# Attention values as plain fp32 products, row sums on VectorE

## The chip, the cores and the metric

The kernel runs on one core of a Trainium2 chip. The metric is the device time of one execution in microseconds (us). The kernel before took 1972.14 us as the median of three runs (1970.95 to 1979.14). The profiled execution took 1971.03 us. The engines are called as the profile calls them: PE is TensorE (PEld its weight loads), DVE is VectorE, ACT is ScalarE, POOL is GpSimd, and SP issues most of the transfers.

## The reference, cut to what matters

Two layers run one after the other on 1024 positions of width 1024. The change lies in the second layer, in a latent attention with 8 heads; everything else is left out here.

```python
def odd_layer(x, cos, sin, g_pre, g_post, w_in, g_q, w_uq, g_kv, w_ukv, w_fd, w_out):
    ...
    k_nope, v = kv[..., :QK_NOPE], kv[..., QK_NOPE:]      # 128 and 128 columns per head
    ...
    def attend(qs):
        qn, qr = qs
        s = jnp.einsum('bqhd,bkhd->bhqk', qn, k_nope) + jnp.einsum('bqhr,bkr->bhqk', qr, k_rope)
        pr = jax.nn.softmax(s.astype(jnp.float32) * scale, axis=-1).astype(v.dtype)
        return jnp.einsum('bhqk,bkhd->bqhd', pr, v)
    ...
    y = jnp.concatenate([y_c, y_d], axis=-1) @ w_out
    return x + rms_norm(y, g_post)
```

## The kernel before

Products of fp32 matrices are made of three products in the type fp32r. Each operand is split into a high part, rounded to fp32r, and a low part, the rest. `mm3` then multiplies high by high, high by low and low by high, all into one sum in PSUM. The split `split_act_dve` is a copy on ACT (the high part) and a subtraction on DVE (the low part); `wload` splits weights on ACT or POOL.

The attention goes through the heads `h` and, for each, through 8 tiles of 128 keys (`kt`). One tile of work is 128 keys by 1024 queries. The loop is skewed: in the pass for head `h` PE makes the scores of head `h` (`scores`), and for the head before, `h - 1`, the exponentials (`weigh`) and the products with the values (`values`) are made. `scores` leaves a score tile in PSUM, which ACT copies to `st` and DVE folds into a running maximum `acc`. After eight tiles `maxima` turns `acc` on PE, reduces it on DVE to `sm`, and spreads it over the partitions as `mb`. `weigh` subtracts `mb` (DVE, line 1741), takes the exponential `e` (ACT, line 1742), adds `e` to the row sums `es` (POOL, lines 1745 and 1747), and splits `e` into `eh` and `el` (ACT line 201, DVE line 202). `values` makes two times three products of 512 columns into the PSUM tiles `c` and `d` (lines 196 to 198). `finish` multiplies by a gate into `zt`, sums `es` over the partitions on PE (line 1772), takes the reciprocal (`rsum`, line 1774), and stores the head's output. `v_page` makes the values of a pair of heads, split into `vh` and `vl`. `prep_q`, `prep_k` and `prep_r` make the queries and keys of the next head; their weights are split on POOL (lines 180 and 181).

For head 7 there are no further scores. The scheduler puts a part of the output projection beside it: products `mm<-wh,yh`, with the splits of its weights on POOL (`wl`, line 210) and of its inputs on DVE (`yl`), and with sums and differences of blocks on DVE (`s`, `a`, `b`, lines 303 and 306) and POOL. The rest of the projection follows, then the last normalization and the stores.

A scheduler with a model of times sets the order on each engine when the kernel is built. Each engine then runs its list in that order, and so does SP with the transfers.

Of the kernel before, what the change touches and what calls it, by code (L numbers as in the profile page):

```python
# [8 lines left out]
F32 = mybir.dt.float32  # L9
F32R = mybir.dt.float32r  # L10
I32 = mybir.dt.int32
BF16 = mybir.dt.bfloat16
AF = mybir.ActivationFunctionType
ALU = mybir.AluOpType
AX = mybir.AxisListType

P = 128
S = 1024
D = 1024
NT = S // P  # L20
# [10 lines left out]
NEG = -(2.0 ** 100)  # L31
SB = 3
ST_BUFS = 9
E_BUFS = 3
ES_BUFS = 1
EH_BUFS = 2
PTS = [6]*7+[2]
EB = 3
CB = 6
# [40 lines left out]
def hybrid_encoder(ctx: ExitStack, tc: tile.TileContext, d):  # L80
    nc = tc.nc
    V, A, PL, T = nc.vector, nc.scalar, nc.gpsimd, nc.tensor
# [23 lines left out]
    def nm(s):  # L106
        uid[0] += 1
        return f"{s}_{uid[0]}"
# [60 lines left out]
    def wload(src, n, bufs=None, pool=None, tags=("wh", "wl")):  # L169

        raw = wr_pool.tile([P, w_cols], F32, tag="wr", name=nm("wr"))[:, :n]
        pool = pool or wpool
        m = w_cols if tags[0] == "wh" else n
        hi = pool.tile([P, m], F32R, tag=tags[0], bufs=bufs, name=nm("wh"))[:, :n]
        lo = pool.tile([P, m], F32R, tag=tags[1], bufs=bufs, name=nm("wl"))[:, :n]
        nc.sync.dma_start(out=raw, in_=src)
        if w_act[0]:
            A.activation(hi, raw, AF.Copy)
        else:
            PL.tensor_scalar(out=hi, in0=raw, scalar1=1.0, scalar2=1.0, op0=ALU.mult, op1=ALU.mult)  # L180
        PL.tensor_tensor(out=lo, in0=raw, in1=f(hi), op=ALU.subtract)
        return hi, lo
# [12 lines left out]
    def mm3(out, lh, ll, rh, rl, start, stop, shared=False):  # L195
        T.matmul(out, lh, rh, start=start, stop=False, skip_group_check=shared)  # L196
        T.matmul(out, lh, rl, start=False, stop=False, skip_group_check=shared)  # L197
        T.matmul(out, ll, rh, start=False, stop=stop, skip_group_check=shared)  # L198

    def split_act_dve(hi, lo, src):  # L200
        A.activation(hi, src, AF.Copy)  # L201
        V.tensor_tensor(out=lo, in0=src, in1=f(hi), op=ALU.subtract)  # L202
# [179 lines left out]
    wv, fu_w = [], []  # L382
# [16 lines left out]
    for half in range(2):  # L399
# [10 lines left out]
        pt = c_tile()  # L410
# [9 lines left out]
        pt = c_tile()  # L420
        for j in range(4):
            T.matmul(pt[:, j * P:(j + 1) * P], rsh[:, 4 * half + j:4 * half + j + 1].broadcast_to([P, P]),
                     ident, start=True, stop=True)
# [711 lines left out]
    for k in range(NK):  # L1135
        pt, g = x1_cols(ysb1, k)
# [8 lines left out]
    for i in range(n):  # L1145
        w = w_load(0, k2[i])
# [477 lines left out]
    def v_page(h, q):  # L1624

        pr = h // 2
        if pr not in wv:
            wv[pr] = (wload(d["wv"][pr * P:(pr + 1) * P, :], 512, 1, None, ("whv", "wlv")), [], [])
        w, vh, vl = wv[pr]
        pt = a_tile()  # L1630
        for j in range(2):
            tt = 2 * q + j
            for k in range(2):
                mm3(pt[:, j * 256:(j + 1) * 256], tt_slices(ckh[k], tt), tt_slices(ckl[k], tt),
                    w[0][:, k * 256:(k + 1) * 256], w[1][:, k * 256:(k + 1) * 256], k == 0, k == 1)
        vh.append(at.tile([P, 512], F32R, tag="vh", bufs=4, name=nm("vh")))
        vl.append(at.tile([P, 512], F32R, tag="vl", bufs=4, name=nm("vl")))
        split_act_dve(vh[q], vl[q], pt)

    def load_w(h, *parts):  # L1640

# [84 lines left out]
            A.activation(mb[:, i * 512:(i + 1) * 512], pt, AF.Copy)  # L1726
        s_["mb"] = mb

    def e_parts(e):
        eh = at.tile([P, S], F32R, tag="eh", bufs=EH_BUFS, name=nm("eh"))  # L1730
        el = at.tile([P, S], F32R, tag="el", bufs=EH_BUFS, name=nm("el"))
        split_act_dve(eh, el, e)
        return eh, el

    def weigh(h, kt):

        s_ = hd[h]
        st = s_["st"][kt]
        sc = st
        st = at.tile([P, S], F32, tag="e", bufs=E_BUFS, name=nm("e"))  # L1740
        V.tensor_tensor(out=st, in0=sc, in1=s_["mb"], op=ALU.subtract)  # L1741
        A.activation(st, st, AF.Exp, scale=scale)  # L1742
        if kt == 0:
            s_["es"] = at.tile([P, S], F32, tag="es", bufs=ES_BUFS, name=nm("es"))
            PL.tensor_scalar(out=s_["es"], in0=st, scalar1=1.0, scalar2=1.0, op0=ALU.mult, op1=ALU.mult)
        else:
            PL.tensor_tensor(out=s_["es"], in0=s_["es"], in1=st, op=ALU.add)  # L1747
        s_["eh"], s_["el"] = e_parts(st)

    def values(h, kt):  # L1750
        s_ = hd[h]
        if kt == 0:
            s_["po"] = [c_tile(), d_tile()]
        _, vh, vl = wv[h // 2]
        vs = slice((kt % 2) * 256 + (h % 2) * P, (kt % 2) * 256 + (h % 2 + 1) * P)
        for i in range(2):
            qs = slice(i * 512, (i + 1) * 512)
            mm3(s_["po"][i], vh[kt // 2][:, vs], vl[kt // 2][:, vs], s_["eh"][:, qs], s_["el"][:, qs],
                kt == 0, kt == NT - 1)

    def finish(h):

# [79 lines left out]
    with ExitStack() as os_:  # L1842
# [10 lines left out]
            return yp.tile([P, 512], F32, tag=tag, bufs=bufs, name=nm(tag))  # L1853

        def junk1():
            return at.tile([P, 512], BF16, tag="vh", bufs=4, name=nm("junk"))


        acc0 = op_acc(0)
# [33 lines left out]
            third(i)  # L1893
        second(n - 1)
        third(n - 1)
        gp1 = at.tile([P, D], F32, tag="eh", bufs=EH_BUFS, name="gp1")
        nc.sync.dma_start(out=gp1, in_=d["g_post1"].broadcast_to([P, D]))
        ss1, ss2 = (small.tile([P, 8], F32, tag="oss", name=nm("oss")) for _ in range(2))
        for j in range(4):
# [31 lines left out]
        for i in range(n):  # L1931
            w = w_load(0, k1[i])
            sub(V, w, b11[i], w)
            t = at.tile([P, S], F32, tag=("el", "el", "eh")[i], bufs=EH_BUFS, name=nm("a22"))
            a22.append([t[:, 0:512], t[:, 512:1024]])
            for r in range(2):
                y_load(2 * k2[i] + r, 1, a22[i][r])
                sub(V, a11[i][r], a22[i][r], a11[i][r])
            block(w, a11[i], acc0, i)
# [22 lines left out]
        for j in range(4):  # L1962
            ts_ = slice(j * P, (j + 1) * P)
            for i in range(n):
                for r in range(2):
                    cs = slice(r * 512, (r + 1) * 512)
                    mm3(acc1[j], ys[i][r][0][:, ts_], ys[i][r][1][:, ts_], ws_[i][0][:, cs], ws_[i][1][:, cs],
                        i + r == 0, i == n - 1 and r == 1)
            t = ysb2[j]
            add(t[:, f0], t[:, f0], acc1[j])  # L1970
            junk = at.tile([P, 512], BF16, tag="vh", bufs=4, name=nm("junk"))
            A.activation(junk, t[:, f0], AF.Square, accum_out=ss2[:, j:j + 1])
            s1 = small.tile([P, 1], F32, tag="oss2", name=nm("oss2"))
            V.tensor_tensor(out=s1, in0=ss2[:, j:j + 1], in1=ss2[:, 4 + j:5 + j], op=ALU.add)
            PL.tensor_tensor(out=t[:, f0], in0=t[:, f0], in1=gp1[:, f0], op=ALU.mult)
            rs = rms_scale(s1, 1, D)
            for cs in (f0, f1):
                V.scalar_tensor_tensor(out=t[:, cs], in0=t[:, cs], scalar=rs, in1=xr[j][:, cs],
                                       op0=ALU.mult, op1=ALU.add)
                nc.scalar.dma_start(out=d["out"][(4 + j) * P:(5 + j) * P, cs], in_=t[:, cs])  # L1980
# [130 lines left out]
```

## Time and profile before

| | |
|---|---|
| median of three runs | 1972.14 us (1970.95 to 1979.14) |
| profiled execution | 1971.03 us |
| its span | 1969.3 us |
| PE busy | 1795.7 us, 91% |
| DVE busy | 1511.4 us, 77% |
| ACT busy | 775.2 us, 39% |
| POOL busy | 759.4 us, 39% |
| chain that ended last | PE 60%, DVE 23%, issue 8%, DMA 5%, POOL 2%, ACT 2% |

The span is the profiled stretch of that execution. Busy shares are averages over stages with different limits, so the stage of the change has to be read by itself. A matmul's record is longer than the time until the next one starts, because matmuls are pipelined; what a matmul costs is read from one start to the next. The granted clock of PE stands as a share of 2.4 GHz; the two levels are 1.2 and 2.4 GHz.

### The profile page before, as it was taken

What the parts mean: (1) busy time and instruction counts of PE and PEld (TensorE: products, weight loads), DVE (VectorE), ACT (ScalarE), POOL (GpSimd) and SP (SyncE); (2) the same over time, 40 slices, a digit from 0 to 9 for tenths busy, and PEclk for the clock granted to TensorE, in tenths of its full rate; (3) what the DMA queues carried; (4) which work ended last, traced back from release to release, by engine and by line L of the source; (5) the groups of instructions that cost most, each with busy time, mean ns of one, the idle gap of its engine ahead of it and who ended that gap; (6) DMA issues with size and microseconds to landing.
All of it is one profiled execution on the core that took longest, in us unless ns stands there. A gap on an engine that the chain in (4) does not pass through costs nothing.

```text
span 1969.3 us, 22736 instructions
## 1 busy us (share of the span) xinstructions
PE 1795.7 (91%) x8204; PEld 1422.6 (72%) x8204; DVE 1511.4 (77%) x2260; ACT 775.2 (39%) x1217; POOL 759.4 (39%) x453
## 2 busy tenths in 40 slices
PE   6999999999999999988967999989989898987786
PEld 6988888888888777766855787768667676665564
DVE  7597757698776257788788879656787978899788
ACT  5322232233232334434455323342555545564232
POOL 3432231323221114127554332331454545467343
PEclk8999999999999999989978999999999999998898
DMA  4333232313312515675235134463001001033423
GB/s 156 119 106 120 75 97 73 99 54 105 112 63 75 192 49 183 218 273 177 86 132 207 59 114 154 146 202 110 13 18 58 15 30 34 32 133 107 155 76 128
DMA packets 99491, 214.34 MB, mean 109 GB/s; under 512 B 10098, under 2 KB 31091, under 8 KB 99251
## 3 DMA queue, kind: packets, MB, share of 16 engines
q1 hardware_dynamic: 66610, 158.69, 24.9%
q10 hardware_dynamic: 32768, 54.21, 7.3%
q8 instruction: 64, 1.05, 0.2%
q14 instruction: 49, 0.39, 0.1%
HBM read 154.47 MB, written 58.39 MB: 108 GB/s over the span
## 4 chain that ended last, share of the span: by engine, by line
PE 60%; DVE 23%; issue 8%; DMA 5%; POOL 2%; ACT 2%; SPq 0%; DVEq 0%; ACTq 0%; POOLq 0%
PE s L198 10%; PE s L196 10%; PE s L197 10%; DVE el L202 4%; DVE e L1741 3%; PE mm L196 2%; PE mm L198 2%; PE mm L197 2%; DVE yl L202 2%; PE p L196 1%; PE p L198 1%; PE p L197 1%; PE p L879 1%; POOL wl L210 1%; PE o L875 1%
## 5 line engine op out<-in xcount | busy, mean ns | idle before, releaser
L618 DVE SCALAR_TENSOR_TENSOR cv<-u,cwh,cv 128x1024 f32<-128x1024 f32 x232 | 298.4, 1286 | 12.4 <-ACT cv L615 8.2
L210 POOL TENSOR_TENSOR wl<-wr,wh 128x1024 fp32r<-128x1024 f32 (+2 forms) x61 | 152.6, 2503 | 229.6 <-ACT wh L209 228.1
L1747 POOL TENSOR_TENSOR es<-es,e 128x1024 f32<-128x1024 f32 x56 | 167.8, 2996 | 74.6 <-ACT e L1742 72.8
L202 DVE TENSOR_TENSOR el<-e,eh 128x1024 fp32r<-128x1024 f32 x64 | 127.9, 2008 | 0.0
L210 POOL TENSOR_TENSOR ql<-raw,qh 128x1024 fp32r<-128x1024 f32 x34 | 81.4, 2399 | 119.0 <-ACT qh L209 119.0
L1741 DVE TENSOR_TENSOR e<-st,mb 128x1024 f32<-128x1024 f32 x64 | 110.7, 1750 | 13.3 <-ACT mb L1726 12.8
L196 PE MATMUL s<-qh,pg 128*128 128x512 f32 x304 | 120.2, 395 | 0.0
L198 PE MATMUL s<-qh,pg 128*128 128x512 f32 x304 | 119.8, 394 | 0.0
L197 PE MATMUL s<-ql,pg 128*128 128x512 f32 x304 | 119.1, 392 | 0.0
L1742 ACT ACTIVATE e<-e 128x1024 f32<-128x1024 f32 x64 | 67.7, 1059 | 101.8 <-DVE e L1741 101.8
L196 PE MATMUL s<-pg,qh 128*128 128x512 f32 x240 | 95.6, 398 | 0.0
L198 PE MATMUL s<-pg,ql 128*128 128x512 f32 x240 | 95.3, 397 | 0.0
L197 PE MATMUL s<-pg,qh 128*128 128x512 f32 x240 | 95.3, 397 | 0.0
L209 ACT ACTIVATE wh<-wr 128x1024 fp32r<-128x1024 f32 (+2 forms) x61 | 58.9, 968 | 64.1 <-DVE wr L303 17.9
L198 PE MATMUL s<-wh,pg 128*128 128x512 f32 (+2 forms) x224 | 79.6, 360 | 2.4 <-DVE pg L372 2.4
L196 PE MATMUL s<-wh,pg 128*128 128x512 f32 (+2 forms) x224 | 80.0, 358 | 0.6 <-ACT wr L607 0.6
L197 PE MATMUL s<-wl,pg 128*128 128x512 f32 (+2 forms) x224 | 79.2, 355 | 0.0
L1700 ACT ACTIVATE st<-mm 128x1024 f32<-128x1024 f32 x64 | 65.1, 1019 | 35.4 <-PE mm L1698 35.3
L209 ACT ACTIVATE qh<-raw 128x1024 fp32r<-128x1024 f32 x34 | 36.0, 1060 | 93.0 <-PE s L197 65.7
L201 ACT ACTIVATE eh<-e 128x1024 fp32r<-128x1024 f32 x64 | 67.0, 1052 | 4.5 <-PE d L198 3.1
L196 PE MATMUL mm<-qh,kh 128*128 128x512 f32 x128 | 56.1, 438 | 12.6 <-DVE acc L1707 12.1
L198 PEld LDWEIGHTS s<-qh,pg 128*128 128x128 f32 x304 | 57.1, 188 | 13.3
(720 smaller groups left out, 5404.8 us busy)
## 6 DMA issues: line engine op xcount, KB each, us to landing
wr<-in_wout_dram SPq DMA_DIRECT2D x47, 512.0 KB, 3.9
wr<-in_w_dram SPq DMA_DIRECT2D x27, 512.0 KB, 3.7
raw<-in_wa_dram SPq DMA_DIRECT2D x22, 512.0 KB, 3.8
pg<-yd SPq DMA_DIRECT2D x40, 256.0 KB, 4.7
raw<-in_woz_dram SPq DMA_DIRECT2D x16, 512.0 KB, 3.6
raw<-in_wkv_dram SPq DMA_DIRECT2D x12, 512.0 KB, 3.5
ud<-pg ACTq DMA_DIRECT2D x19, 256.0 KB, 4.6
a<-yd SPq DMA_DIRECT2D x18, 256.0 KB, 5.2
```

The source lines that it names most:

```text
L196: T.matmul(out, lh, rh, start=start, stop=False, skip_group_check=shared)
L197: T.matmul(out, lh, rl, start=False, stop=False, skip_group_check=shared)
L198: T.matmul(out, ll, rh, start=False, stop=stop, skip_group_check=shared)
L201: A.activation(hi, src, AF.Copy)
L202: V.tensor_tensor(out=lo, in0=src, in1=f(hi), op=ALU.subtract)
L209: A.activation(hi, src, AF.Copy)
L210: PL.tensor_tensor(out=lo, in0=src, in1=f(hi), op=ALU.subtract)
L618: tap = V.scalar_tensor_tensor(out=cv if k < TAPS - 1 else acc, in0=u[:, k:k + S], scalar=cwh[:, g, k:k + 1], in1=cv, op0=ALU.mult, op1=AL ...
L1700: A.activation(st, ps, AF.Copy)
L1741: V.tensor_tensor(out=st, in0=sc, in1=s_["mb"], op=ALU.subtract)
L1742: A.activation(st, st, AF.Exp, scale=scale)
L1747: PL.tensor_tensor(out=s_["es"], in0=s_["es"], in1=st, op=ALU.add)
```

## The change

The exponentials and the values are no longer split. `v_page` keeps one fp32 tile `v` (one copy on ACT; before, a copy on ACT and a subtraction on DVE). `values` makes one product of fp32 operands where there were three of fp32r. The copy `eh` on ACT and the subtraction `el` on DVE go. The row sums `es` move from POOL to DVE; the first of them adds the first two tiles, so there are seven per head where POOL had a copy and seven additions. `e` has five buffers where it had three; `eh` and `el` had two each. Four tiles of the output projection that used the space of `eh` and `el` (`gp1` and three of `a22`) get other places.

```diff
-E_BUFS = 3
+E_BUFS = 5
...
-        vh.append(at.tile([P, 512], F32R, tag="vh", bufs=4, name=nm("vh")))
-        vl.append(at.tile([P, 512], F32R, tag="vl", bufs=4, name=nm("vl")))
-        split_act_dve(vh[q], vl[q], pt)
+        v.append(at.tile([P, 512], F32, tag="vh", bufs=8, name=nm("v")))
+        A.activation(v[q], pt, AF.Copy)
...
         if kt == 0:
             s_["es"] = at.tile([P, S], F32, tag="es", bufs=ES_BUFS, name=nm("es"))
-            PL.tensor_scalar(out=s_["es"], in0=st, scalar1=1.0, scalar2=1.0, op0=ALU.mult, op1=ALU.mult)
+            s_["e0"] = st
         else:
-            PL.tensor_tensor(out=s_["es"], in0=s_["es"], in1=st, op=ALU.add)
-        s_["eh"], s_["el"] = e_parts(st)
+            V.tensor_tensor(out=s_["es"], in0=s_["e0"] if kt == 1 else s_["es"], in1=st, op=ALU.add)
+        s_["e"] = st
...
-            mm3(s_["po"][i], vh[kt // 2][:, vs], vl[kt // 2][:, vs], s_["eh"][:, qs], s_["el"][:, qs],
-                kt == 0, kt == NT - 1)
+            T.matmul(s_["po"][i], v[kt // 2][:, vs], s_["e"][:, qs], start=kt == 0, stop=kt == NT - 1)
...
-        gp1 = at.tile([P, D], F32, tag="eh", bufs=EH_BUFS, name="gp1")
+        gp1 = at.tile([P, D], F32, tag="gp", bufs=1, name="gp1")
...
-            t = at.tile([P, S], F32, tag=("el", "el", "eh")[i], bufs=EH_BUFS, name=nm("a22"))
+            t = at.tile([P, S], F32, tag="e", bufs=E_BUFS, name=nm("a22"))
```

The lists of all engines are the same up to the first values of the attention. From there the scheduler orders them anew. The numbers behind a name say which tile it is. In the changed kernel the line numbers are lower by up to nine.

First DVE's list where the weighing of head 4 starts, right behind the second reduction of its maxima. Before:

```order
L1720 TENSOR_REDUCE sm_2327_13095<-a_2330_13098 128x4
L202 TENSOR_TENSOR ql_2359_13226<-mm_2360_13227,qh_2358_13225 128x1024
L1741 TENSOR_TENSOR e_2346_13179<-st_2255_12744,mb_2328_13096 128x1024
L1741 TENSOR_TENSOR e_2355_13211<-st_2263_12774,mb_2328_13096 128x1024
L1741 TENSOR_TENSOR e_2366_13268<-st_2281_12855,mb_2328_13096 128x1024
L202 TENSOR_TENSOR kl_2335_13129<-a_2333_13121,kh_2334_13128 128x512
L1774 RECIPROCAL rsum_2341_13151<-a_2340_13142 128x8
L1705 TENSOR_TENSOR acc_2354_13209<-st_2345_13177,mm_2352_13196 128x1024
L202 TENSOR_TENSOR el_2349_13185<-e_2346_13179,eh_2348_13184 128x1024
L1781 TENSOR_TENSOR zt_2339_13138<-zt_2339_13138,a_2342_13153 128x512
L1781 TENSOR_TENSOR zt_2339_13138<-zt_2339_13138,a_2343_13159 128x512
L1707 TENSOR_TENSOR acc_2354_13209<-acc_2354_13209,mm_2364_13254 128x1024
```

And with the change, at the same place (L1733 is the subtraction of `mb`, L1739 the row sum, L1703 and L1705 are the running maximum):

```order
L1718 TENSOR_REDUCE sm_2251_12811<-a_2254_12814 128x4
L201 TENSOR_TENSOR ql_2279_12925<-mm_2280_12926,qh_2278_12924 128x1024
L1733 TENSOR_TENSOR e_2270_12895<-st_2199_12533,mb_2252_12812 128x1024
L1733 TENSOR_TENSOR e_2277_12918<-st_2205_12554,mb_2252_12812 128x1024
L1733 TENSOR_TENSOR e_2286_12967<-st_2220_12625,mb_2252_12812 128x1024
L1733 TENSOR_TENSOR e_2289_12987<-st_2223_12645,mb_2252_12812 128x1024
L1733 TENSOR_TENSOR e_2292_13007<-st_2228_12680,mb_2252_12812 128x1024
L201 TENSOR_TENSOR kl_2259_12845<-a_2257_12837,kh_2258_12844 128x512
L1765 RECIPROCAL rsum_2265_12867<-a_2264_12858 128x8
L1703 TENSOR_TENSOR acc_2276_12916<-st_2269_12893,mm_2274_12903 128x1024
L1739 TENSOR_TENSOR es_2271_12898<-e_2270_12895,e_2277_12918 128x1024
L1705 TENSOR_TENSOR acc_2276_12916<-acc_2276_12916,mm_2284_12953 128x1024
```

Five subtractions now stand ahead of the first maximum of the next head, where three stood; the `el` behind it is a row sum now.

PE's list in the same pass, where the first products with the values stand. Before, the end of a score tile (`mm`) and the second half of a values tile, which needs `el`:

```order
L1695 MATMUL mm_2374_13310<-qrt_2301_12956,krh_10499 128x512
L1698 MATMUL mm_2374_13310<-qrt_2301_12956,krl_10500 128x512 x2
L197 MATMUL c_2350_13188<-el_2357_13216,vh_2272_12811 128x512
L198 MATMUL c_2350_13188<-eh_2356_13215,vl_2273_12812 128x512
L197 MATMUL d_2351_13189<-el_2357_13216,vh_2272_12811 128x512
L198 MATMUL d_2351_13189<-eh_2356_13215,vl_2273_12812 128x512
L196 MATMUL c_2350_13188<-eh_2367_13272,vh_2291_12913 128x512
```

With the change (L1750 is the product with the values, L1771 the spreading of the reciprocals):

```order
L1696 MATMUL mm_2284_12953<-qrt_2233_12700,krl_10500 128x512 x2
L1750 MATMUL c_2272_12899<-e_2270_12895,v_2212_12583 128x512
L1750 MATMUL d_2273_12900<-e_2270_12895,v_2212_12583 128x512
L1750 MATMUL c_2272_12899<-e_2277_12918,v_2212_12583 128x512
L1750 MATMUL d_2273_12900<-e_2277_12918,v_2212_12583 128x512
L1750 MATMUL c_2272_12899<-e_2286_12967,v_2226_12667 128x512
L1750 MATMUL d_2273_12900<-e_2286_12967,v_2226_12667 128x512
L1771 MATMUL a_2266_12869<-cst_81,rsum_2265_12867 128x128 x4
L1771 MATMUL a_2267_12875<-cst_81,rsum_2265_12867 128x128 x4
```

Three tiles of values (six products) now stand together, with no score tile between them.

Last, DVE's list in the weighing of head 7, beside the output projection. Before:

```order
L202 TENSOR_TENSOR el_2569_14263<-e_2567_14258,eh_2568_14262 128x1024
L303 TENSOR_TENSOR a2_2634_14526<-a2_2634_14526,a1_2594_14384 128x512
L202 TENSOR_TENSOR el_2572_14277<-e_2570_14272,eh_2571_14276 128x1024
L202 TENSOR_TENSOR yl_2658_14624<-s_2655_14618,yh_2657_14623 128x512
L1741 TENSOR_TENSOR e_2576_14300<-st_2533_14100,mb_2548_14174 128x1024
L202 TENSOR_TENSOR yl_2662_14634<-s_2659_14628,yh_2661_14633 128x512
L303 TENSOR_TENSOR b_2601_14422<-wr_2663_14662,b_2601_14422 128x1024
L1741 TENSOR_TENSOR e_2579_14314<-st_2538_14128,mb_2548_14174 128x1024
L306 TENSOR_TENSOR s_2667_14672<-s_2667_14672,s_2668_14674 128x512
L202 TENSOR_TENSOR el_2575_14291<-e_2573_14286,eh_2574_14290 128x1024
L303 TENSOR_TENSOR a1_2602_14424<-s_2667_14672,a1_2602_14424 128x512
L1741 TENSOR_TENSOR e_2582_14328<-st_2543_14156,mb_2548_14174 128x1024
```

With the change (L302 and L305 are differences and sums of the projection):

```order
L305 TENSOR_TENSOR s_14066<-s_14066,s_14068 128x512
L1739 TENSOR_TENSOR es_13743<-es_13743,e_13754 128x1024
L1733 TENSOR_TENSOR e_13772<-st_13637,mb_13687 128x1024
L201 TENSOR_TENSOR yl_13987<-a_2490_13974,yh_13986 128x512
L1733 TENSOR_TENSOR e_13778<-st_13657,mb_13687 128x1024
L1772 TENSOR_TENSOR zt_13712<-zt_13712,a_13727 128x512
L302 TENSOR_TENSOR a_2449_13830<-s_14066,a_2449_13830 128x512
L1772 TENSOR_TENSOR zt_13712<-zt_13712,a_13733 128x512
L1739 TENSOR_TENSOR es_13743<-es_13743,e_13760 128x1024
L305 TENSOR_TENSOR s_14076<-s_14076,s_14078 128x512
L1733 TENSOR_TENSOR e_13784<-st_13677,mb_13687 128x1024
L302 TENSOR_TENSOR b_13828<-wr_14056,b_13828 128x1024
```

Here too `es` stands where `el` stood, with the projection's steps between. Over this stage PE's list holds 93 products of the projection ahead of its last products with the values and the spreading of the reciprocals, where it held 122; the other 29 stand behind.

## Rows read from the trace of the kernel before

**Rows 1.** The page: busy time of four engines.

```profile
PE 1795.7 (91%) x8204; PEld 1422.6 (72%) x8204; DVE 1511.4 (77%) x2260; ACT 775.2 (39%) x1217; POOL 759.4 (39%) x453
```

**Rows 2.** Busy time of each engine by stretch, with granted clock and DMA share.

```profile
core 0: us, PE busy (x) PEld busy (x) DVE busy (x) ACT busy (x) POOL busy (x), PEclk, DMA share, GB/s
...
1403.50:1757.00 353.50, 316.60 (x1471) 232.05 (x1470) 309.62 (x245) 196.35 (x223) 196.31 (x106) 0.97 0.11 36
1757.00:1844.00 87.00, 62.59 (x242) 48.23 (x241) 82.78 (x60) 35.35 (x46) 55.08 (x19) 0.81 0.42 138
1844.00:1946.00 102.00, 86.21 (x353) 68.29 (x352) 79.93 (x97) 37.67 (x71) 45.41 (x21) 0.95 0.35 122
```

**Rows 3.** Waits of PE in 1403.5 to 1757: total, times, longest.

```profile
PE c L197 <- DVE el L202: 16.0, 14, 1.8
PE mm L196 <- DVE acc L1707: 12.1, 5, 4.1
PE c L196 <- ACT eh L201: 4.0, 3, 1.9
```

**Rows 4.** DVE's costliest groups in 1403.5 to 1757.

```profile
L202 DVE TENSOR_TENSOR el<-e,eh 128x1024 fp32r<-128x1024 f32 x55 | 109.5, 2002 | 0.0
L1741 DVE TENSOR_TENSOR e<-st,mb 128x1024 f32<-128x1024 f32 x56 | 98.9, 1787 | 13.3 <-ACT mb L1726 12.8
```

**Rows 5.** Instructions on tile `e`, all of the program: shortest, median, longest, ns.

```profile
L1741 DVE TENSOR_TENSOR e<-st,mb x64: 1206/1225/3423, 1403.6 to 1821.1; 128x1024 f32<-128x1024 f32 x64
...
L202 DVE TENSOR_TENSOR el<-e,eh x64: 1209/1569/3436, 1411.0 to 1835.8; 128x1024 fp32r<-128x1024 f32 x64
L1747 POOL TENSOR_TENSOR es<-es,e x56: 2348/3242/4096, 1410.4 to 1823.6; 128x1024 f32<-128x1024 f32 x56
```

**Rows 6.** Timeline of PE in the first layer: plain fp32 products, 257 columns.

```profile
706.27 0.60 PE L879 MATMUL p<-v,kw 128*128 128x257 f32 x2
706.70 0.60 PE L874 MATMUL o<-C,kw 128*128 128x257 f32 x2
707.13 0.60 PE L875 MATMUL o<-v,pg 128*128 128x257 f32 x2
```

**Rows 7.** Timeline of PE: fp32r products of 512 columns, then sums of `es`.

```profile
1561.40 0.39 PE L197 MATMUL mm<-cql,wh 128*128 128x512 f32 x1
...
1564.43 0.39 PE L198 MATMUL a<-ckh,wl 128*128 128x512 f32 x1
1564.67 1.84 PE L1772 MATMUL a<-one,es 128*128 128x1 f32 x16
```

**Rows 8.** Timeline of DVE with POOL idle: one wide step, two narrow ones.

```profile
1787.28 1.21 DVE L202 TENSOR_TENSOR el<-e,eh 128x1024 fp32r<-128x1024 f32 x1
1788.41 0.68 DVE L202 TENSOR_TENSOR yl<-a,yh 128x512 fp32r<-128x512 f32 x1
1789.01 0.68 DVE L306 TENSOR_TENSOR s<-s,s 128x512 f32<-128x512 f32 x1
```

**Rows 9.** DVE's costliest groups in 1757 to 1844.

```profile
L202 DVE TENSOR_TENSOR el<-e,eh 128x1024 fp32r<-128x1024 f32 x10 | 21.0, 2101 | 0.0
L202 DVE TENSOR_TENSOR yl<-a,yh 128x512 fp32r<-128x512 f32 x11 | 16.8, 1555 | 0.0
L1741 DVE TENSOR_TENSOR e<-st,mb 128x1024 f32<-128x1024 f32 x8 | 11.7, 1488 | 0.0
```

**Rows 10.** POOL's groups in 1757 to 1844.

```profile
L1747 POOL TENSOR_TENSOR es<-es,e 128x1024 f32<-128x1024 f32 x8 | 22.2, 2769 | 10.2 <-ACT e L1742 10.1
L210 POOL TENSOR_TENSOR wl<-b,wh 128x1024 fp32r<-128x1024 f32 x5 | 16.2, 3261 | 0.0
L210 POOL TENSOR_TENSOR wl<-wr,wh 128x1024 fp32r<-128x1024 f32 x3 | 10.2, 3385 | 7.1 <-ACT wh L209 7.1
L303 POOL TENSOR_TENSOR b<-wr,b 128x1024 f32<-128x1024 f32 x2 | 6.2, 3089 | 0.0
```

**Rows 11.** The page: one kind of transfers, median us from issue to landing.

```profile
a<-yd SPq DMA_DIRECT2D x18, 256.0 KB, 5.2
```

More of the change, by code (lines that the diff above doesn't have):

```diff
@@ L33 @@
 ST_BUFS = 9
-E_BUFS = 3
+E_BUFS = 5
 ES_BUFS = 1
-EH_BUFS = 2
 PTS = [6]*7+[2]
@@ L1627, in v_page @@
         if pr not in wv:
-            wv[pr] = (wload(d["wv"][pr * P:(pr + 1) * P, :], 512, 1, None, ("whv", "wlv")), [], [])
-        w, vh, vl = wv[pr]
+            wv[pr] = (wload(d["wv"][pr * P:(pr + 1) * P, :], 512, 1, None, ("whv", "wlv")), [])
+        w, v = wv[pr]
         pt = a_tile()
@@ L1727, in maxima @@
         s_["mb"] = mb
[L1729 to L1733, printed above, removed]
     def weigh(h, kt):
@@ L1753, in values @@
             s_["po"] = [c_tile(), d_tile()]
-        _, vh, vl = wv[h // 2]
+        _, v = wv[h // 2]
         vs = slice((kt % 2) * 256 + (h % 2) * P, (kt % 2) * 256 + (h % 2 + 1) * P)
@@ L1855, in junk1 @@
         def junk1():
-            return at.tile([P, 512], BF16, tag="vh", bufs=4, name=nm("junk"))
+            return at.tile([P, 512], BF16, tag="vh", bufs=8, name=nm("junk"))
         acc0 = op_acc(0)
@@ L1970, in hybrid_encoder @@
             add(t[:, f0], t[:, f0], acc1[j])
-            junk = at.tile([P, 512], BF16, tag="vh", bufs=4, name=nm("junk"))
+            junk = at.tile([P, 512], BF16, tag="vh", bufs=8, name=nm("junk"))
             A.activation(junk, t[:, f0], AF.Square, accum_out=ss2[:, j:j + 1])
```

## Prediction

> **What bounds the kernel now.** I read the page first, then the busy times by stage, then PE's waits in the stage of the change, then the groups of DVE and POOL there. The page names PE as the busiest engine, with 91% of the span, ahead of DVE with 77% [rows 1]. That average says little about the attention. The lists of all engines are equal up to the first values of the attention, so only what lies behind about 1403 us of the span can change, and I split it at the places where the work changes its kind [rows 2].
>
> In the first stage, 353.5 us in which heads 0 to 6 are weighed while the next head's scores are made, PE is busy 316.6 us and DVE 309.6 us. Neither is free, and neither is full. PE loses 36.9 us there, and the three largest waits are for `el` (16.0 us), for the running maximum `acc` (12.1 us) and for `eh` (4.0 us), all but the last of them on DVE [rows 3]. The granted clock is 0.97; at two levels of 1.2 and 2.4 GHz that is 6% of the time at the lower, and half of that, 10.6 us, is lost. DVE itself is not busy with honest work: a subtraction `el` or `e` of 1024 columns can take 1.21 us, but in this stage they take 2.00 and 1.79 us on the mean [rows 4, 5]. The long ones, 3.4 us, are as much above the short ones as one of POOL's additions `es` takes at the least, 2.35 us; the two engines hold each other up.
>
> In the second stage, 87.0 us for head 7 beside the output projection, DVE is the bound: 82.8 us busy, PE 62.6 us, at a granted clock of 0.81 [rows 2]. In the third, 102 us, PE is busy 86.2 us at 0.95, so it is nearly the bound there, and what is moved into that stage costs its PE time.
>
> **The products with the values.** A product of fp32r with 512 columns costs 0.233 us from start to start: the two rows shown stand 13 products apart, in 3.03 us [rows 7]. Three make 0.70 us. The trace has no plain fp32 product of 512 columns. It has some of 257: each stands as two records, and the next starts 0.43 us later [rows 6]. By columns, 0.43 x 512 / 257 = 0.86 us. The lower bound is two fp32r products, 0.47 us, if the long form were cheaper by column than the short one; nothing speaks for it, since a column costs 1.67 ns in the row, four times the 0.42 ns of a cycle at 2.4 GHz, and no fixed part is left over. The upper bound is four times the fp32r product, 0.93 us. I take 0.86 us: a product with the values becomes 0.16 us dearer, 128 of them 20 us, about 110 of them (18 us) in the first stage. On PE by itself the change is a loss.
>
> The Trainium skill, FP8 and Floating Point Precision, under TensorE Precision Notes, says that true fp32 takes four passes through the array, where the kernel now makes three; it speaks against the change. By it, with the row's 0.233 us for a pass, the products cost 30 us more in all instead of 20, and the forecast comes out some 9 us later. The trace agrees on four cycles a column; it shows nothing of 512 columns.
>
> **DVE and POOL in the first stage.** DVE loses 55 `el` of 109.5 us in all [rows 4]. It gets 49 row sums. With POOL idle a wide step follows the next after 1.13 us [rows 8], so these cost 55.4 us. POOL loses all its `es` steps, of which one takes 2.35 us at the least and 3.24 us in the median [rows 5], so nothing of length is left beside DVE but the weight splits of the next head. The 56 `e` then go from 98.9 us to 56 x 1.13 = 63.3 us. DVE's sum is 309.6 - 109.5 + 55.4 - 35.6 = 220 us. At the other end, if `e` and `es` took the 1.79 us of today, it would be 309.6 - 109.5 + 87.7 = 288 us; I take the first, since POOL is what the long ones stand beside. In both cases DVE is below PE and no longer the bound.
>
> PE's work at full clock is 316.6 - 10.6 = 306 us, with the products 324 us. What waits stay? The one for `el` goes with `el`, and the chain from `e` to the product is two steps shorter. What is late next is `acc`: in DVE's list five `e` now stand ahead of the next head's first maximum, where three stood. Behind that maximum stand PE's next score tiles, since it frees their place in PSUM. From `mb` on it takes DVE 5 x 1.13 + 1.13 (`ql`) + 0.6 (`kl`) + 0.1 + 1.13 = 8.6 us. PE has in that time the sums of `es`, a score tile and the six products with the values that now stand together, 1.8 [rows 7], ten products or 2.3, and 6 x 0.86 = 5.2: 9.3 us. It fits, barely. So I leave 10 us of the 36.9 as waits, and half of the lost clock, 5 us: 324 + 10 + 5 = 339 us, 14 us less than today. The bounds: no wait and full clock, 324 us, a gain of 29; all waits and the same clock, 353.5 + 18, a loss of 18.
>
> **The second stage.** Here I count DVE's list. Today it holds 20 wide and 38 narrow steps, and two reciprocals: 20 x 1.13 + 38 x 0.6 + 0.4 = 45.8 us when nothing is beside them [rows 8, 9]. They take 82.8 us, so 37 us are put on by POOL, which is busy 55.1 us [rows 2]. With the change DVE has 17 wide steps (8 `e`, 7 `es`, 2 `b`) and 29 narrow ones up to the end of the head, some of the projection's going behind it: 19.2 + 17.4 + 1.4 for the reductions and reciprocals = 38 us. POOL keeps the weights of the projection, 16.2 + 10.2 + 6.2 = 32.6 us, and loses the rest [rows 10]. I scale what POOL puts on by its time: 37 x 32.6 / 55.1 = 22 us. With the 4.2 us that DVE idles today the stage takes 38 + 22 + 4 = 64 us, 23 less. But 29 products of the projection now stand behind it, 29 x 0.233 = 6.8 us in the third stage, where PE counts. That leaves 16 us. The bounds: POOL puts on as much as today, 79 us, a gain of 1 after the products moved; POOL puts on so little that PE's own work sets the end, by estimate 93 x 0.233 + 16 x 0.86 + some 10 for the small products = 45 us, a gain of 35.
>
> **What costs nothing.** ACT loses `eh` and was busy 196 of 353.5 us [rows 2]. The early load of `gp1` and the other places of `a22` lie in five buffers of `e` that the attention has left by then; without that cover such a load would land 5.2 us late, once [rows 11].
>
> **The sum.** 14 + 16 = 30 us off the profiled execution's 1971.0 us: 1941 us. The median of the runs shown lies 1.1 us above that execution, less than I can tell.
>
> **The rivals.** *PE's waits go altogether.* The relieved DVE is always early: first stage 324 us, second stage some 7 us better than my sum. That is 1971.0 - 29 - 23 = 1919 us. DVE's 220 us against PE's 324 speak for it; the five `e` in a row speak against.
>
> *The dearer products eat the first stage.* PE's waits move from `el` to `e` and `acc` by about as much as they shrink, so the first stage gives 0 to 5 us, the second 10: 1956 to 1961 us, and with less from the second stage no change that can be told. For it: PE works 306 of 353.5 us already and gets 18 more. Against: the 16.0 us behind `el` have no successor as long.
>
> *The burst of `e` stalls PE.* This one ends on the other side. If the first maximum's 8.6 us lay bare at each of 6.6 heads, that is 57 us of waits; the first stage takes 324 + 57 + 5 = 386 us, 32 more, and with 16 from the second stage the time is 1988 us. It decides from about 6.2 us of waits for each head (41 us in all: 324 + 41 + 5 = 370 us, which cancels the 16). For it: `acc` is PE's second largest wait already, up to 4.1 us at once [rows 3], and the weight splits on POOL fall into the same microseconds. Against: PE's list puts the six products into that gap.
>
> *The form isn't what it seems.* If a plain fp32 product of 512 columns were a single pass of 0.23 us, PE would be 128 x 0.63 = 80 us lighter than in my sum, and the time would fall below 1905 us; the two records of the row speak against it.
>
> **How the numbers follow.** My forecast, 1925 to 1956 us, gets 0.55; all waits gone, 1905 to 1925 us, 0.18, with the cheap form in it; the first stage eaten 0.20, half of it above 1962 us and so no change; the burst 0.07. A measurement of this kernel can tell about 0.5%, 10 us, from no change. So faster has 0.83, same 0.10, slower 0.07. For 8 in 10, I leave out half of the case below and most above 1965 us: 1914 to 1965 us.
>
> **What would show it.** In the profile after: 256 records of the new product, 0.43 us from one to the next (more, and the skill's four passes are nearer). `e` and `es` on DVE near 1.2 us in the first stage, with DVE near 220 us there. PE's wait for `e` or `acc` at 10 us in all, with a clock above 0.97. The end of head 7 some 23 us sooner after the last maxima than the 87 us of today, with POOL's weight splits still drawing DVE's steps there to 3 us. The prediction is wrong if the products take over 0.9 us, if PE waits for `acc` at each head for over 6 us, or if the second stage stays long because the projection's loads, in a new order on SP, come late.

## The result, and the profile after

The changed kernel takes 1918.38 us, the median of four runs (1912.88 to 1920.84), against 1971.55 us before; the ratio is 0.9718 (95% interval 0.9684 to 0.9753). The forecast was 1941 us in a range of 1914 to 1965; the result lies 4 us above its lower end. The profiled execution took 1920.8 us, 50.2 us less than the profiled one of before.

The page of the changed kernel, its span and its busy times, answers to [rows 1]:

```profile
span 1919.0 us, 22204 instructions
...
PE 1792.7 (93%) x8076; PEld 1392.6 (73%) x8076; DVE 1419.2 (74%) x2236; ACT 714.2 (37%) x1153; POOL 582.6 (30%) x389
```

PE works nearly as long as before, and all the others less. By stage, split as in [rows 2] (from the start of the first exponentials to the last maxima, to the end of head 7, and then to the last instruction):

```profile
core 0: us, PE busy (x) PEld busy (x) DVE busy (x) ACT busy (x) POOL busy (x), PEclk, DMA share, GB/s
...
1403.50:1734.00 330.50, 325.11 (x1391) 213.65 (x1390) 239.22 (x232) 146.22 (x172) 45.45 (x51) 0.99 0.11 39
1734.00:1788.00 54.00, 52.82 (x196) 38.60 (x196) 48.45 (x49) 23.82 (x33) 19.08 (x6) 0.85 0.56 200
...
1788.00:1919.00 131.00, 97.28 (x394) 77.28 (x392) 111.74 (x170) 42.10 (x81) 63.65 (x30) 0.89 0.32 115
```

The first stage went from 353.5 to 330.5 us, the second from 87.0 to 54.0 us, and what follows from 125.3 (1844.0 to 1969.3) to 131.0 us: 23.0 + 33.0 - 5.7 = 50.3 us. In the first stage PE idles 5.4 us where it idled 36.9, at a granted clock of 0.99. Its waits there, against [rows 3]:

```profile
PE a L195 <- POOL wh L179: 2.7, 1, 2.7
PE a L1716 <- DVE acc L1705: 2.4, 1, 2.4
PE a L1722 <- DVE sm L1718: 0.3, 1, 0.3
```

None of them is a wait for an exponential, and none comes back at every head. DVE's groups in the same stretch, against [rows 4]:

```profile
L1733 DVE TENSOR_TENSOR e<-st,mb 128x1024 f32<-128x1024 f32 x56 | 75.6, 1400 | 26.3 <-ACT mb L1724 26.3
L1739 DVE TENSOR_TENSOR es<-es,e 128x1024 f32<-128x1024 f32 x42 | 51.5, 1226 | 0.9
L1705 DVE TENSOR_TENSOR acc<-acc,mm 128x1024 f32<-128x1024 f32 x42 | 51.1, 1217 | 34.8 <-ACT st L1698 34.8
```

The sums cost what a step costs without POOL beside it, 1.23 us, and DVE now waits for score tiles, 34.8 us ahead of `acc`: it is early. The products with the values, in PE's timeline inside one head:

```profile
1653.06 1.02 PE L1750 MATMUL d<-e,v 128*128 128x512 f32 x2
1653.92 1.02 PE L1750 MATMUL c<-e,v 128*128 128x512 f32 x2
1654.78 1.02 PE L1750 MATMUL d<-e,v 128*128 128x512 f32 x2
```

Each is two records, and the next starts 0.86 us later.

### The profile page after: what moved, and what is told of

Same layout as the page of the kernel before. It is cut to its first block, busy times and chain, and to the rows that moved or that the text cites. A ratio compares the mean times of both kernels' runs of the same rounds, so it can differ in the third digit from the quotient of the medians.

```text
span 1919.0 us, 22204 instructions
## 1 busy us (share of the span) xinstructions
PE 1792.7 (93%) x8076; PEld 1392.6 (73%) x8076; DVE 1419.2 (74%) x2236; ACT 714.2 (37%) x1153; POOL 582.6 (30%) x389
## 4 chain that ended last, share of the span: by engine, by line
PE 71%; DVE 15%; issue 5%; DMA 4%; POOL 2%; ACT 2%; SPq 0%; DVEq 0%; ACTq 0%; POOLq 0%
PE s L197 10%; PE s L195 10%; PE s L196 10%; PE mm L195 4%; PE mm L196 3%; PE mm L197 3%; PE c L1750 3%; PE d L1750 3%; PE mm L1693 2%; PE mm L1696 1%; DVE yl L201 1%; PE a L195 1%; PE p L197 1%; PE p L195 1%; PE p L878 1%
## 5 line engine op out<-in xcount | busy, mean ns | idle before, releaser
L1733 DVE TENSOR_TENSOR e<-st,mb 128x1024 f32<-128x1024 f32 x64 | 89.4, 1445 | 27.6 <-ACT mb L1724 27.6
L1705 DVE TENSOR_TENSOR acc<-acc,mm 128x1024 f32<-128x1024 f32 x48 | 58.4, 1217 | 41.3 <-ACT st L1698 41.3
L1673 POOL TENSOR_SCALAR qd<-qr 128x256 f32<-128x256 f32 x32 | 14.3, 464 | 192.9 <-PE a L1677 163.9
L1750 PE MATMUL c<-e,v 128*128 128x512 f32 x128 | 68.6, 618 | 0.0
L196 PEld LDWEIGHTS s<-ql,pg 128*128 128x128 f32 x304 | 57.1, 188 | 12.8
```

The lines of the kernel that those rows point to most:

```text
L1705: V.tensor_tensor(out=s_["acc"], in0=s_["acc"], in1=ps, op=ALU.max)
L1750: T.matmul(s_["po"][i], v[kt // 2][:, vs], s_["e"][:, qs], start=kt == 0, stop=kt == NT - 1)
```

## The experiments

Each of the kernels e1 to e9 was timed together with seven runs of the kernel before on the same chip; the ratios are to that. The medians of the kernel before were 1968.89 to 1970.87 us there, so medians of different rows can differ by 2 us for that alone. To compare stages across kernels whose lists differ, I split each trace at the first and the last copy of `mb` (the start of the first and the last head's exponentials) and at the last multiplication of `zt` (the end of the attention). For the changed kernel these rows give the three times, 1403.9, 1735.6 and 1787.4 us:

```profile
L1724 ACT ACTIVATE mb<-a x16: 590/597/599, 1403.9 to 1735.6; 128x512 f32<-128x512 f32 x16
```

```profile
L1772 DVE TENSOR_TENSOR zt<-zt,a x16: 670/679/682, 1472.5 to 1787.4; 128x512 f32<-128x512 f32 x16
```

| kernel | heads 0 to 6 | head 7 | after it | median, ratio (95%) |
|---|---|---|---|---|
| before | 360.0 | 82.4 | 124.4 | 1971.55 |
| changed | 331.7 | 51.8 | 131.6 | 1918.38, 0.9718 (0.9684 to 0.9753) |
| e1, sums alone to DVE | 353.2 | 63.5 | 124.2 | 1943.61, 0.9865 (0.9850 to 0.9880) |
| e2, sums left on POOL | 333.7 | 57.3 | 132.5 | 1923.07, 0.9767 (0.9748 to 0.9786) |
| e3, products twice | 424.3 | 45.6 | 144.1 | 2018.36, 1.0246 (1.0229 to 1.0263) |
| e4, three buffers of e | 334.8 | 61.7 | 125.5 | 1926.82, 0.9780 (0.9765 to 0.9795) |
| e5, one fp32r pass | 315.9 | 61.5 | 119.3 | 1903.19, 0.9670 (0.9654 to 0.9686) |
| e6, two fp32r passes | 309.7 | 59.3 | 116.3 | 1891.45, 0.9616 (0.9596 to 0.9635) |
| e7, idle subtraction | 358.3 | 61.6 | 121.7 | 1944.82, 0.9876 (0.9862 to 0.9891) |
| e8, half of them | 333.8 | 67.3 | 118.8 | 1928.37, 0.9782 (0.9765 to 0.9798) |
| e9, e6 with three buffers | 334.5 | 58.2 | 120.5 | 1918.19, 0.9732 (0.9717 to 0.9747) |

The stages are of one profiled execution each, in us, and what precedes them differs by up to 10 us between profiles (the first `mb` comes between 1398.8 and 1409.2 us). Nor do the stages hold the same work: the scheduler moves products of the projection over their borders. In head 7 PE has 222 records before (16 of them due to the form of the products), 186 in the changed kernel, 196 in e1, 214 in e4 and e7, 235 in e8. So head 7 is best read together with what follows: 206.8 us before, 183.4 changed, 187.7 in e1, 189.8 in e2, 187.2 in e4, 183.3 in e7, 186.1 in e8.

**e1_sums_on_dve.** One part of the change alone, on the kernel before:

```diff
-            PL.tensor_scalar(out=s_["es"], in0=st, scalar1=1.0, scalar2=1.0, op0=ALU.mult, op1=ALU.mult)
+            s_["e0"] = st
         else:
-            PL.tensor_tensor(out=s_["es"], in0=s_["es"], in1=st, op=ALU.add)
+            V.tensor_tensor(out=s_["es"], in0=s_["e0"] if kt == 1 else s_["es"], in1=st, op=ALU.add)
         s_["eh"], s_["el"] = e_parts(st)
```

> The kernel before, with its splits into high and low parts, and only the row sums moved from POOL to DVE (seven per head). Theory P (POOL's sums were the brake: they hold up DVE's steps, so PE waits): el and e fall from 2.0 and 1.8 us to about 1.2 us, DVE has 309.6 - 47 - 36 + 55 = 282 us of work in the first stage, and most of the gain is there: 1935 to 1950 us. Theory L (the low part was the brake: el on DVE and the two steps between e and the product): el stays, DVE gets 55 us more to do, and nothing is gained: 1965 to 1985 us.

1943.61 us, half of the gain. Its first stage, and two of DVE's groups there:

```profile
1403.00:1754.00 351.00, 325.06 (x1529) 244.66 (x1528) 312.13 (x304) 207.32 (x237) 61.48 (x54) 0.97 0.14 47
```

```profile
L1741 DVE TENSOR_TENSOR e<-st,mb 128x1024 f32<-128x1024 f32 x55 | 69.9, 1298 | 8.7 <-ACT mb L1726 8.7
L202 DVE TENSOR_TENSOR el<-e,eh 128x1024 fp32r<-128x1024 f32 x56 | 69.4, 1249 | 0.8 <-ACT eh L201 0.7
```

The steps did shrink to 1.25 and 1.30 us, as theory P has it, and the total lies in its range. But DVE is as busy as before, 312 us where P had 282: `e` and `el` lost 69 us together, and the sums (63 us) and eight steps of the projection that now run here (11 us) filled that. So the first stage gave 7 us, though it also holds some of the projection's products, and head 7 gave 19 us. P put most of the gain into the first stage, and theory L had none at all: neither fits alone.

**e2_sums_on_pool.** The other part alone, the changed kernel with the sums as they were:

```diff
-            s_["e0"] = st
+            PL.tensor_scalar(out=s_["es"], in0=st, scalar1=1.0, scalar2=1.0, op0=ALU.mult, op1=ALU.mult)
         else:
-            V.tensor_tensor(out=s_["es"], in0=s_["e0"] if kt == 1 else s_["es"], in1=st, op=ALU.add)
+            PL.tensor_tensor(out=s_["es"], in0=s_["es"], in1=st, op=ALU.add)
```

> The changed kernel with the row sums back on POOL, a copy and seven additions per head. Theory P: POOL holds up e again (1.8 us in place of 1.4), and a good part of the gain is lost: 1945 us or more. Theory L: e alone keeps ahead of PE even at 1.8 us, since DVE loses the sums (60 us of 239 in the first stage), so the first stage stays at 330 to 335 us, and only the second stage, where DVE is full, gets 5 to 15 us longer: 1920 to 1935 us.

1923.07 us: nearly all of the gain, as theory L has it; the interval of its ratio overlaps that of the changed kernel. Its first stage, and DVE's `e` there:

```profile
1401.00:1733.00 332.00, 325.61 (x1388) 213.24 (x1388) 208.58 (x184) 146.25 (x171) 197.58 (x107) 0.99 0.12 41
```

```profile
L1733 DVE TENSOR_TENSOR e<-st,mb 128x1024 f32<-128x1024 f32 x56 | 102.7, 1886 | 47.4 <-ACT mb L1724 40.6 <-POOL es L1739 6.9
```

An `e` takes 1.89 us, longer than before the change, and PE is full all the same. So a longer step does not make PE wait by itself; what is left as the cause is DVE's sum, 209 us here, or the place of `el` in the chain; e7 tells these two apart. Mainly head 7 pays, 57.3 us against 51.8: PE waits there for an exponential once for 5.6 us.

**e3_products_twice.** Values halved, every product made twice:

```diff
-        A.activation(v[q], pt, AF.Copy)
+        A.activation(v[q], pt, AF.Copy, scale=0.5)
...
-            T.matmul(s_["po"][i], v[kt // 2][:, vs], s_["e"][:, qs], start=kt == 0, stop=kt == NT - 1)
+            for r in range(2):
+                T.matmul(s_["po"][i], v[kt // 2][:, vs], s_["e"][:, qs], start=kt == 0 and r == 0,
+                         stop=kt == NT - 1 and r == 1)
```

> The changed kernel with values halved and every product with the values made twice into the same sum: 128 products of 0.86 us more, 110 us, about 96 of them in the first stage. If PE is the bound in the attention, the time grows by nearly all of it: 2015 to 2030 us. If something else sets the pace there (e, the maxima, the exponentials), PE's extra work hides behind it in part: under 2000 us.

2018.36 us, 100 us over the changed kernel, as expected with PE as the bound. Its first stage:

```profile
1402.00:1824.00 422.00, 418.74 (x1617) 254.23 (x1615) 238.56 (x233) 148.60 (x173) 43.38 (x52) 1.00 0.10 33
```

The first stage grew by 92.6 us for 112 products more, 0.83 us each; that is a little under 0.86, since PE also idles 2 us less and the granted clock is 1.00 instead of 0.99. PE is the bound of the changed kernel's first stage, and work added to it costs its full time there. So the dearer products cost what the prediction's sum has for them, some 18 us; they were paid out of a larger gain.

**e4_three_e_buffers.** The depth of `e` as before, with buffers of their own for `a22`:

```diff
-E_BUFS = 5
+E_BUFS = 3
...
-            t = at.tile([P, S], F32, tag="e", bufs=E_BUFS, name=nm("a22"))
+            t = at.tile([P, S], F32, tag="x22", bufs=3, name=nm("a22"))
```

> The changed kernel with three buffers of e in place of five, and the projection's three tiles a22 in buffers of their own; the scheduler makes a new order, with at most three subtractions in a row. If the burst of five e is what costs waits (my rival of the prediction), PE waits less than the 5.4 us of now, and the time is 1910 to 1918 us. If the depth is what keeps PE fed, PE waits for e, and the time is 1925 to 1950 us. If neither, 1915 to 1922 us.

1926.82 us. The first stage is 3.1 us longer, head 7 is 9.9 us longer, what follows 6.1 us shorter; head 7 holds 28 records of PE more, so most of these last two is work that moved. PE's longest wait in head 7 is for the end of the chain of sums:

```profile
PE a L1763 <- DVE es L1739: 5.0, 1, 5.0
```

The time lies in the range that I gave to the depth as what feeds PE, but not for that reason: PE waits for exponentials for 0.6 us in the first stage and 2.5 us in head 7. So the burst of five `e` doesn't hurt; that the depth helps head 7 is not shown, since the order and the places of `a22` changed with it. In the changed kernel the burst can be seen at one head:

```profile
1648.27 6.50 DVE L1733 TENSOR_TENSOR e<-st,mb 128x1024 f32<-128x1024 f32 x5 [5.75 <-ACT mb L1724]
1654.68 1.21 DVE L201 TENSOR_TENSOR ql<-mm,qh 128x1024 fp32r<-128x1024 f32 x1
1655.82 0.19 DVE L1765 RECIPROCAL rsum<-a 128x8 f32<-128x8 f32 x1
1655.93 1.16 DVE L1703 TENSOR_TENSOR acc<-st,mm 128x1024 f32<-128x1024 f32 x1
```

Here the first maximum ends 8.8 us after the burst starts, and PE is at its six products with the values up to 1657 us. Over the seven heads of the stage it is 7.6 to 9.9 us, and no wait of PE for this maximum is in the list of its waits.

**e7_idle_subtraction and e8_half_the_idle_subtractions.** Work for DVE that nothing reads, at every tile, or (e8, under `if kt % 2:`) at every second:

```diff
         s_["e"] = st
+        jd = at.tile([P, S], F32, tag="jd", bufs=1, name=nm("jd"))
+        V.tensor_tensor(out=jd, in0=st, in1=s_["mb"], op=ALU.subtract)
```

> The changed kernel with one more subtraction of 1024 columns on DVE for each tile, from e into a tile that nothing reads: 64 steps, 72 us, as much DVE work as el took at its shortest, but not between e and the product. DVE then has 239 + 63 = 302 us in the first stage, nearly the 309.6 of the kernel before. If el's place in the chain before the product was what PE waited for, PE stays fed and the first stage stays at 330 to 336 us, with the second some 5 us longer: 1920 to 1930 us. If el's work on DVE was what counted, PE waits again and the time goes to that of the run with the sums alone on DVE: 1938 to 1950 us.

1944.82 us, as expected if `el`'s work on DVE was what counted. The first stage of e7, DVE's two longest waits there, and PE's longest:

```profile
1402.00:1759.00 357.00, 338.79 (x1408) 220.93 (x1406) 307.07 (x294) 150.75 (x178) 62.53 (x53) 0.96 0.14 46
```

```profile
DVE e L1733 <- ACT mb L1724: 40.0, 7, 5.8
DVE sm L1718 <- PE a L1716: 12.2, 6, 2.8
PE mm L195 <- DVE acc L1705: 8.5, 6, 2.8
```

The first stage is back at 358.3 us although `el` is gone from the chain. DVE waits almost only at the change of heads, for the maxima, which it cannot run ahead of; all the rest of the time it is busy. The idle step also holds `e` a little longer, but PE has no wait for an `e` here: it waits for the running maximum, which is late on DVE. Of the 27 us by which the stage is longer than in the changed kernel, PE's idle time makes 13 (18.2 us against 5.4), and the granted clock of 0.96 against 0.99 makes some 11, by estimate (0.04 x 357 less 0.01 x 330.5). From this, and before e8, theory M: the first stage is as long as the longer of PE's work and DVE's busy time with its 40 to 50 us of idle time at the changes of head.

> The run with the idle subtraction, but only for every second tile: 28 steps in the first stage, 32 us more for DVE. Theory M (the first stage is as long as the longer of two: PE's work with some 5 us of waits, 331 us, or DVE's busy time with the 40 to 50 us in which it waits for the maxima of each new head): DVE comes to 239 + 34 + 45 = 318 us, below PE's 331, so the first stage stays at 331 to 336 us, and the time at 1918 to 1928 us. Theory W (waits grow in step with DVE's load): half of the 27 us that the whole of the subtractions added to the first stage, 345 us, and 1929 to 1935 us.

```profile
1404.00:1738.00 334.00, 327.12 (x1399) 214.32 (x1397) 265.43 (x257) 143.37 (x168) 42.80 (x50) 0.99 0.10 35
```

For the first stage theory M holds: 333.8 us, 2.1 more than without the idle work, where theory W had 345. The total of 1928.37 us lies between the two expectations. Head 7 took 67.3 us, but with 49 records of PE more in it, and what follows is 12.8 us shorter; both together are 2.7 us longer than in the changed kernel. Another 5.3 us of the profiled execution lie before the first `mb`, in a part that the edit does not touch.

**e5_one_pass and e6_two_passes.** Both round the exponentials to fp32r and so leave out their low part; e5 leaves out that of the values too. The subtraction now writes into the score tile, which is so held until the exponential has read it. The core of the edit, and (last two lines) of e6:

```diff
-        st = at.tile([P, S], F32, tag="e", bufs=E_BUFS, name=nm("e"))
-        V.tensor_tensor(out=st, in0=sc, in1=s_["mb"], op=ALU.subtract)
-        A.activation(st, st, AF.Exp, scale=scale)
+        st = at.tile([P, S], F32R, tag="e", bufs=E_BUFS, name=nm("e"))
+        V.tensor_tensor(out=sc, in0=sc, in1=s_["mb"], op=ALU.subtract)
+        A.activation(st, sc, AF.Exp, scale=scale)
...
+            T.matmul(s_["po"][i], v[kt // 2][:, vs], s_["e"][:, qs], start=kt == 0, stop=False)
+            T.matmul(s_["po"][i], vl[kt // 2][:, vs], s_["e"][:, qs], start=False, stop=kt == NT - 1)
```

> The changed kernel with the exponentials and the values rounded to fp32r (the low parts of both are left out), so that a product with the values is one fp32r product of 0.233 us in place of 0.86 us: 128 x 0.63 = 80 us less for PE, about 70 in the first stage. PE's work there would be 322 - 70 = 252 us, DVE's is 239 us. If PE was the only bound and DVE follows, the first stage takes some 270 us and the kernel 1850 to 1865 us. If something behind PE (e, the exponentials, the maxima at each head's start) is close, half of it stays: 1875 to 1895 us.

> The changed kernel with the exponentials rounded to fp32r (their low part is left out) and the values in high and low parts: two fp32r products of 0.233 us in place of one plain one of 0.86 us, 128 x 0.39 = 50 us less for PE, and 16 narrow subtractions for vl on DVE (11 us). PE as the bound: 44 us less in the first stage, 1870 to 1882 us. If DVE is close behind: 1885 to 1900 us.

1903.19 us and 1891.45 us. e6 lies in its second range, DVE close behind; e5 lies above both of its ranges. Both gain, both less than PE's work alone would give, and e5, with the least work, is the slower one. PE's longest waits in the first stage of e5 and the busy times there, and the same of e6:

```profile
PE mm L195 <- DVE ql L201: 15.4, 6, 3.1
PE c L1750 <- ACT e L1734: 11.4, 18, 1.1
PE mm L195 <- DVE acc L1705: 5.1, 7, 2.0
```

```profile
1405.00:1720.00 315.00, 276.65 (x1279) 198.15 (x1278) 238.84 (x233) 145.98 (x171) 53.26 (x51) 0.92 0.13 43
```

```profile
PE mm L195 <- DVE ql L201: 6.3, 3, 2.3
PE c L1751 <- ACT e L1735: 3.8, 8, 0.8
```

```profile
1404.00:1713.00 309.00, 287.67 (x1390) 212.76 (x1389) 245.40 (x245) 147.15 (x174) 48.55 (x52) 0.98 0.13 43
```

In e5 PE idles 38 us, mostly for `ql` and `acc`, which stand behind `e` on DVE, and for the exponentials; its granted clock is 0.92, which by itself takes some 25 us, by estimate (0.08 x 315). It met other limits before it got to its 252 us of work. In e6 PE idles 21 us (287.67 of 309 us), at 0.98.

**e9_two_passes_three_buffers.** e6 with the edit of e4.

> The run with two passes (the low part of the exponentials is left out) with three buffers of e in place of five and buffers of their own for the projection's a22. In the run with two passes PE still waits 6.3 us for ql, which stands behind five e on DVE. If that burst costs, three in a row shorten the first stage by up to 6 us: 1880 to 1889 us. If, as with plain products, the second stage gets longer by more than the third gains: 1893 to 1902 us.

1918.19 us, some 25 us slower than e6, and outside what I expected. Its two longest waits of PE in the first stage:

```profile
PE mm L195 <- DVE ql L201: 16.1, 4, 4.7
PE a L1773 <- DVE rsum L1767: 13.3, 3, 4.9
```

With three buffers the new order puts `ql` and the reciprocals later on DVE than PE wants them. The edit that cost 3 us of the first stage with plain products costs 25 us of it here: PE idles 36.5 us instead of 21, and the granted clock is 0.94 instead of 0.98. The fastest of all the kernels is e6, which rounds the exponentials.

## Why the prediction was right, and where it was too small

**The direction and the mechanism held.** The products became dearer for PE and yet the kernel got faster, since DVE's relief was worth more. The product costs 0.86 us as worked out by columns from [rows 6]. By the four passes that the Trainium skill states in FP8 and Floating Point Precision, TensorE Precision Notes, each priced as one of this kernel's fp32r products, it would be 0.93 us, an estimate; the measured row lies below that, at 1.68 ns a column, four times the 0.42 ns of a cycle at 2.4 GHz. DVE's busy time in the first stage is 239 us where I had 220: the `e` take 1.40 us, not 1.13, in part because some run beside POOL's weight splits (the longest takes 2.3 us), in part because I took the spacing where the duration counts.

**The forecast took the wrong case for the likeliest.** What came is nearest to my first rival, PE's waits go altogether, 1919 us. That the total agrees with it to 1 us is luck: it had 324 us for the first stage, which took 330.5, and 57 us for the second, which took 54.0. The step that was mis-sized in the first stage is "So I leave 10 us of the 36.9 as waits, and half of the lost clock, 5 us": 5.4 us stayed, and at 0.99 some 3 us of clock. The reading behind it, "Neither is free, and neither is full", was wrong. DVE was full but for the changes of head. Its 309.6 us of [rows 2] left 43.9 us idle, and its longer waits there, in the kernel before, all lie in the last 15 us ahead of the first `e` of a head:

```profile
DVE sm L1720 <- PE a L1718: 14.8, 9, 3.2
DVE e L1741 <- ACT mb L1726: 12.8, 5, 5.7
DVE zt L1768 <- PE c L198: 10.7, 6, 3.9
DVE ql L202 <- ACT qh L201: 10.0, 2, 5.0
```

The first two are the maxima, the third is for the last products of a head, which need `el` themselves, and the last is for queries that are being made. e1, with 312 us, leaves 39, and e7, with 307 us, leaves 50, and all three first stages are 353 to 360 us long from `mb` to `mb`. With DVE at 265 us or less (e8, the changed kernel, e2) the stage is 332 to 334 us, PE's work. That busy and idle time add up to the stage says nothing by itself; what counts is that the waits at the changes of head did not shrink when e7 gave DVE more to do, so that the stage had to grow. These runs also show that DVE's load, not the place of `el` before the product, set the pace: e7 has no `el` in the chain and is as slow. In PE's terms the stage lost 31.5 us of idle time and some 7 us at the lower clock (0.03 x 353.5 less 0.01 x 330.5, an estimate) and got 16 us of work more: 23 us. My rival of the burst fell: the 8.6 us were 7.6 to 9.9 us, and PE had work enough meanwhile at every head.

**The second stage was mis-sized too.** I had 64 us and 16 net; it took 54.0 us. The step is "POOL keeps the weights of the projection": it kept 19.1 us of the 32.6, the rest ran later. My scaling would have given 37 x 19.1 / 55.1 = 13 us put on DVE. DVE's 48.45 us, less some 38 for its list, leave 10. So the rule of scaling was about right and its input was not. But DVE's list, on which the sum of 64 us stood, is not what sets the end there: PE does, busy 52.82 of 54 us. At its clock of 0.85 that is some 44.7 us of work at full clock, by estimate (52.82 less 0.15 x 54), near the prediction's bound of 45 us. Of the 33 us gained, 23 are idle time of PE (24.4 us before, 1.2 after) and some 8 are clock (0.19 x 87 less 0.15 x 54), a term that the sum for this stage did not have. What follows grew by 5.7 us where I had put 6.8 us of products behind the stage; the nearness is luck: between the last `mb` and the last `zt` 107 products of the projection ran, not the 93 counted, and behind the stage PE has only 394 records instead of 387. The row of before and PE's longest wait there after:

```profile
1844.00:1969.30 125.30, 94.44 (x387) 74.68 (x386) 99.09 (x165) 40.45 (x79) 54.41 (x27) 0.91 0.33 116
```

```profile
PE mm L195 <- DVE ysb L305: 6.0, 1, 6.0
```

PE is busy 2.8 us longer and idle 2.9 us longer there.

**Of the two parts**, the removal of the split gives nearly all (e2: 47 us), the sums on DVE alone half (e1: 27 us), and together they give 53 us. They aren't additive, and most of that lies behind the first stage: there e1 gives 7 us, e2 26 and both 28, while head 7 and what follows give 19, 17 and 23. In head 7 of the changed kernel PE is busy nearly throughout, so relief of DVE beyond that has nothing to give; that this alone explains the rest is not shown.

**What stays open.** Why e5's clock fell to 0.92 while e6's stayed at 0.98 was not tried apart; it waits more often, but the order of its list differs too. Nor did I fix the scheduler's order in any run, so e9's loss may lie in that order rather than in the depth of `e`. The granted clock in head 7 was 0.81 before and 0.85 after. In the changed kernel it falls right behind the wait for the last maxima (PE is busy 3.27 of the 6 us from 1728 to 1734), and once more from 1776 to 1782 us (0.56). No run was made to change that:

```profile
1728.00:1734.00 6.00, 3.27 (x19) 2.33 (x18) 4.01 (x5) 3.21 (x5) 2.35 (x1) 0.96 0.55 197
1734.00:1740.00 6.00, 6.00 (x25) 5.49 (x25) 4.62 (x4) 4.89 (x7) 2.47 (x1) 0.50 1.00 352
1740.00:1746.00 6.00, 6.00 (x20) 4.75 (x19) 6.00 (x4) 3.47 (x6) 2.86 (x1) 0.69 0.62 237
```

At 0.50 PE runs at 1.2 GHz throughout.

## What to carry to other kernels

An engine that is busy nine tenths of a stage can be its bound if the rest is idle time that it cannot use, such as the waits at each change of head here: compare its busy time with the stage less that idle time, not with the stage. When two engines stand that close, taking work off the one may pay even if the other gets more to do; in the first stage here the new length was that of the other one, with hardly any waits. PE's waits cost more than their own length here, since the granted clock fell with them. A step made longer by another engine cost nothing as long as the engine that ran it had room (e2's first stage).

## What the runs showed of the hardware

A plain fp32 product of 512 columns starts 0.86 us after the one before it, as two records, 3.7 times an fp32r product's 0.233 us. So one of them is dearer than three fp32r products by 0.16 us, and two fp32r products are cheaper than it by 0.39 us.
